# First stage rebuilt: six loads on ScalarE's queue, a tied filter chain, and all four quarters of v ahead of the gate products

## The chip, the cores and the metric

The kernel runs on one core of one Trainium2 chip. The metric is the device time of one execution in microseconds (us), the median of several runs. The engines are named as in the profile: PE (TensorE), DVE (VectorE), ACT (ScalarE), POOL (GpSimd) and SP (SyncE, which here only issues DMAs). A DMA is issued by an engine's queue; its data moves on the core's 16 DMA engines.

## The reference, cut to what matters

One layer works on 640 tokens (128 of context, 512 of a latent grid) of width 1024. What the first stage of the kernel computes is this:

```python
mod = (silu(cond) @ ada_w + ada_b)              # shift1, scale1, gate1, shift2, scale2, gate2
h = x * (1.0 + scale1) + shift1
proj = h @ w_in                                  # q, f_fwd, f_bwd, i_raw, g_raw, hy, mg
q, f_fwd, f_bwd, i_raw, g_raw, hy, mg = split(proj)
o_a = hgrn2_mixer(q, f_fwd, f_bwd, i_raw, ...)   # v = heads(i_raw)
o_b = hyena_mixer(hy, p, row_len)                # long convolution by FFT filters
# hyena_filters: h = sin(freq * (h @ w + b)) three times, then h @ w4, times a window
gate_a, gate_b = split(sigmoid(mg))
mix = (gate_a * (o_a @ proj_a) + gate_b * (o_b @ proj_b)) @ w_out
x = layer_norm(ALPHA * x + gate1 * mix)          # then a SwiGLU with shift2, scale2, gate2
```

## The kernel before, in words

All matrix products of fp32 data are made of two parts: a value is split into a high part (a cast) and a low part (the rest), and a product takes three passes of PE (high by high, low by high, high by low). Names that end in h and l are such pairs: hTh and hTl of the modulated input h, wh and wl of a tile of weights, abh and abl, kth and ktl. The weights come in a stream: `issue` loads a raw tile of 512 KB on SP's queue, casts the high part (by the engine that the string HIE names) and subtracts for the low part (by the one that WSUB names in the first stage), three tiles in flight; LOOK says how far ahead of a unit of work its weights are prepared.

The function `start` writes the first stage in the order of the tokens of PLAN; a scheduler then places each instruction on its engine, in order there. The tokens: x0 to x4 load the five blocks of 128 tokens (tile xs) and T0 to T4 transpose them on PE. `mlp` is the filter network, three layers of a small matmul (f1, f2, f3, lines L495, L500, L506) with a sine behind each (a chain of DVE steps on tiles sa and sk, then the sine on ACT, L170). k0 to k2 load a table kt and split it into kth and ktl. L0 to L3 load the weights (w4) and the window (win) of one quarter of the filters; A is `kern_a`: ks matmuls (L543), products with the window on DVE (af), and the split into abh (ACT) and abl (POOL or DVE). B is `kern_b`: matmuls kp and k (L572, L585) against kth and ktl, whose results go to tiles ko by DVE and ACT and are stored by W. D0 to D3 load the modulation's weights, each as two tiles of 1 MB (araw, three buffers), and M0 to M3 multiply and finish them (ada, adaT, modT). h0 to h7 make hTh and hTl. V0 and V1 are `v_unit`: one quarter of v is 120 matmuls of 256 columns (L708). e0 and e2 are `m1_operands`: sums and differences of the h tiles on DVE (mb) and their low parts (m4l to m7l), for products in the Winograd manner. `g0` and the tokens behind it make these gate products (ma, mb, mc, L668), whose weights (rm) are added and split on DVE and ACT as well (wmg0h, wmg0l, wma0l, wmu0l and so on).

Before, two quarters of v are made in the first stage and two (v2 v3 in HGSEQ) in the stage of the HGRN mixer. All loads of the first stage are issued by SP, small parameters by POOL, and the rows of c and c_ctx come with the parameters in one tile prow2. `ada_mods` is placed at high priority. A DMA's completion is counted in one of eight slots, DMAHW0 to DMAHW7, which are given round robin to the DMAs of SP's and ACT's queues; a DMA whose slot is still held waits at its issue until the earlier DMA has landed.

## Time and profile before

| | us |
|---|---|
| median of 3 runs | 1432.4 (1431.38 to 1432.75) |
| the profiled execution | 1434.48 |
| its span in the profile | 1431.4, at a granted PE clock of 0.993 |
| PE busy, DVE busy, ACT busy, POOL busy | 1379.5, 992.7, 620.5, 63.5 |

The profiled execution is 2.1 us above the median, and its span is 3.1 us below its own time. PE is busy for 96% of the span, so that 52 us are left in which it waits; a stage costs what its PE work takes and what PE waits there. Busy times of matmuls overlap, and the time that one really adds is the distance between two starts.

### The profile page before, as it was taken

The numbers are of one execution on the slowest core, as the hardware profiler recorded it, in microseconds if no ns is written. First come the engines' busy times: TensorE is split into PE (matmuls) and PEld (weight loads), VectorE is DVE, ScalarE is ACT, GpSimd is POOL, SyncE is SP. The second block draws the span as 40 slices with busy tenths as digits, with TensorE's granted clock in tenths as the row PEclk, the third lists the DMA queues.
The fourth block names the chain that finished last, engine by engine and source line by source line (L and its number), as shares of the span: only waits on it lengthen the run. The fifth ranks groups of instructions, "written<-read, shape, count | busy, mean of one in ns | idle before, by whom it ended". The sixth has DMA issues, their size and how long they took to land. (4 is left out here: it accounts for less than half of the span.)

```text
span 1431.4 us, 23426 instructions
## 1 busy us (share of the span) xinstructions
PE 1379.5 (96%) x9513; PEld 1294.7 (90%) x9513; DVE 992.7 (69%) x1751; ACT 620.5 (43%) x1011; POOL 63.5 (4%) x56
## 2 busy tenths in 40 slices
...
GB/s 239 334 140 141 207 212 183 199 247 162 93 97 102 113 230 142 144 84 81 76 95 62 68 68 139 221 115 78 88 132 116 78 116 108 83 189 281 74 60 74
DMA packets 198855, 195.63 MB, mean 137 GB/s; under 512 B 7581, under 2 KB 155773, under 8 KB 197980
## 3 DMA queue, kind: packets, MB, share of 16 engines
...
## 5 line engine op out<-in xcount | busy, mean ns | idle before, releaser
L181 DVE TENSOR_TENSOR wl<-raw,wh 128x1024 fp32r<-128x1024 f32 x96 | 117.2, 1223 | 132.9 <-ACT wh L357 132.0
L357 ACT CAST wh<-raw 128x1024 fp32r<-128x1024 f32 x90 | 94.2, 1049 | 221.2 <-PE pb L611 40.9
L1424 PE MATMUL fo<-wh,act 128*128 128x512 f32 (+1 forms) x440 | 130.6, 380 | 0.0
L1424 PEld LDWEIGHTS fo<-wh,act 128*128 128x128 f32 x440 | 81.2, 188 | 15.9
L1424 PE MATMUL fo<-wl,act 128*128 128x512 f32 (+1 forms) x220 | 83.4, 379 | 0.0
L611 PE MATMUL hy<-hTh,wh 128*128 128x320 f32 x256 | 79.6, 311 | 0.0
L611 PE MATMUL hy<-hTh,wl 128*128 128x320 f32 x256 | 79.1, 309 | 0.0
L611 PE MATMUL hy<-hTl,wh 128*128 128x320 f32 x256 | 79.1, 309 | 0.0
L611 PE MATMUL f<-hTh,wh 128*128 128x320 f32 x224 | 70.7, 316 | 0.0
L611 PE MATMUL f<-hTl,wh 128*128 128x320 f32 x224 | 69.7, 311 | 0.0
L611 PE MATMUL f<-hTh,wl 128*128 128x320 f32 x224 | 69.2, 309 | 0.0
L181 POOL TENSOR_TENSOR y<-y,gb 128x512 f32<-128x512 f32 x8 | 11.6, 1452 | 907.4 <-ACT y L170 907.1
L1424 PEld LDWEIGHTS fo<-wl,act 128*128 128x128 f32 x220 | 41.3, 188 | 7.9
L611 PEld LDWEIGHTS hy<-hTh,wh 128*128 128x128 f32 x256 | 48.1, 188 | 0.0
L611 PEld LDWEIGHTS hy<-hTl,wh 128*128 128x128 f32 x256 | 48.1, 188 | 0.0
L611 PEld LDWEIGHTS hy<-hTh,wl 128*128 128x128 f32 x256 | 48.1, 188 | 0.0
L170 ACT ACT_TABLE_LOAD x36 | 46.2, 1283 | 1.4 <-PEq L1770 0.7
L708 PE MATMUL v<-wl,hTh 128*128 128x256 f32 x160 | 45.2, 286 | 1.6 <-DVE wl L181 1.6
L708 PE MATMUL v<-wh,hTl 128*128 128x256 f32 x160 | 45.3, 285 | 0.1
L708 PE MATMUL v<-wh,hTh 128*128 128x256 f32 x160 | 45.1, 286 | 0.0
L611 PEld LDWEIGHTS f<-hTl,wh 128*128 128x128 f32 x224 | 42.2, 188 | 0.0
L611 PEld LDWEIGHTS f<-hTh,wh 128*128 128x128 f32 x224 | 42.2, 188 | 0.0
...
## 6 DMA issues: line engine op xcount, KB each, us to landing
...
```

Source lines behind the costliest of these rows:

```text
L170: r = S.activation(out, in_, func, bias=bias, scale=scale)
L181: return (eng or V).tensor_tensor(out=out, in0=a, in1=b, op=op)
L357: (V.tensor_copy if HIE[i] == "V" else S.copy)(hi, raw)
L611: r = PE.matmul(ps[:, 0:HT], w[a][:, k, :], x[b][:, k, c0:c0 + HT], start=k == 0 and i == 0, stop=k == kt - 1 and i == 2)
L708: PE.matmul(ps[:, (t - t0) * 256:(t - t0) * 256 + 256], hT[b][:, k, t * P:t * P + P], w[a][:, k % 4, :], start=k == 0 and i == 0, stop=k = ...
L1424: PE.matmul(ps, x(t, b, k0 + kk), w[a][:, kk, :], start=first and kk == 0 and i == 0, stop=last and kk == nk - 1 and i == 2)
```

## The change

In the first stage, blocks 0, 4 and 3 of x and three of the eight modulation tiles (a0, a1 and a4; a token a now loads one tile of 1 MB) are issued by ScalarE's queue, and so are the rows of c and c_ctx, in a tile crow that is transposed on its own (`cond_T`). Three instructions are tied in order to a place in the filter network's chain, without a wait: the first modulation matmul behind f3, the first of the two operations on w4 behind the clamp of the second layer, and the casts of kth behind the last sine. All casts of kth and of the first stage's weights are ACT's, all low parts of these weights DVE's. The modulation's multiplications (M) and its finish (Y) are tokens of their own, at no special priority. All four quarters of v stand in the first stage, among the quarters of the filters, and none in the HGRN stage. The tiles ko lie in the buffers of araw and xs, and no longer in those of the weights.

```diff
-PLAN = """x0 k0 L0 k1 x4 k2 p mlp t L1 T0 x3 T4 A0 x2 D0 T2 A1 x1 L2 B0 M0 T1 D2 A2 M2 T3 h0 L3 B1 D1 A3 h1 B2 M1 D3 h2 h3 M3 h4 W2 W0 h5 h6 h7 W1 q V0 e0 B3 g0 W3 V1 m w0 e2 ..."""
-HMOD = "SVSSVSSS"
+PLAN = """x0 a0 x4 a1 x3 a4 c mlp L0 k0 k1 p t T0 T4 T3 x1 x2 k2 a5 M0 M1 Y0 A0 L1 a2 M4 M5 Y2 T1 T2 a3 a6 B0 M2 M3 Y1 a7 h0 h1 h2 h3 A1 M6 M7 Y3 h4 h5 h6 h7 V0 W0 L2 B1 A2 V1 W1 L3 B2 V2 A3 W2 q B3 e0 g0 W3 V3 m w0 e2 ..."""
+HMOD = "SSSSSSSS"
-WSUB = "VGGVVGGG"
+WSUB = "VVVVVVVVVVVV"
...
-HIE = """SSSSVVSVSVSSSSSSSVVVSVVSVSSVSSSS..."""
-LOOK = """2222201220210220112012211122222..."""
+HIE = """SSSSSSSSVVSVSVSSSSSSSVVVSVVSVSSV..."""
+LOOK = """2222222220122021022011201221112..."""
-HGSEQ = """a0 b0 q0 g0 e0 v2 v3 a1 b1 q1 g1 s0 e1 ..."""
+HGSEQ = """a0 b0 q0 g0 e0 a1 b1 q1 g1 s0 e1 ..."""
...
-COPIES = {..., 'k': 'VSS', ...}
+COPIES = {..., 'k': 'SSS', ...}
...
     def tt(out, a, b, op, eng=None):
         return (eng or V).tensor_tensor(out=out, in0=a, in1=b, op=op)
+
+    def order_after(ins, prev):
+        if prev is not None:
+            tc.add_manual_dep(
+                ins.ins, prev.ins.name,
+                mybir.DependencyInfo(mybir.DependencyClass.NoSync, mybir.DependencyReason.DATA),
+                reason="issue order")
     def cpy(which, i, out, in_):
...
     prow1 = sp.tile([P, P], F32, name="prow1")
-    prow2 = sp.tile([65, P], F32, name="prow2")
+    prow2 = sp.tile([49, P], F32, name="prow2")
+    crow = sp.tile([16, P], F32, name="crow")
+    S.dma_start(crow[0:8], I["c_ctx"].rearrange("(k p) -> k p", p=P))
+    S.dma_start(crow[8:16], I["c"].rearrange("o (k p) -> (o k) p", p=P))
     skp_all = sp.tile([1, D], F32, name="skp_all")
     def params_load():
-        G.dma_start(prow2[49:57], I["c_ctx"].rearrange("(k p) -> k p", p=P))
-        G.dma_start(prow2[57:65], I["c"].rearrange("o (k p) -> (o k) p", p=P))
         G.dma_start(skp_all, I["hy_skip"])
...
         G.dma_start(msk, I["msk"])
-    def params_T():
-        ps = tr_bank("pr3_ps")
-        PE.transpose(ps[:, 0:65], prow2, ident[0:65, 0:65])
-        V.tensor_copy(cT.rearrange("p a k -> p (a k)"), ps[:, 49:65])
+    def cond_T():
+        ps = tr_bank("pr2_ps")
+        PE.transpose(ps[:, 0:16], crow, ident[0:16, 0:16])
+        V.tensor_copy(cT.rearrange("p a k -> p (a k)"), ps[:, 0:16])
         act(csig, cT, AF.Sigmoid)
...
             tt(scT[:, :, a:a + 1].rearrange("p k a -> p a k"), cT[:, a:a + 1, :], csig[:, a:a + 1, :], ALU.mult)
+
+    def params_T():
+        ps = tr_bank("pr3_ps")
+        PE.transpose(ps[:, 0:49], prow2, ident[0:49, 0:49])
         V.tensor_copy(prT2, ps[:, 0:49])
...
     modT = cp.tile([P, 4, KT, 2], F32, name="modT")
     ada = dict(raw={}, ps={})
+    net = {}
     def ada_load(nb, i, q, tag, bufs, eng=SY):
...
         for g in range(4):
-            PE.matmul(ps[32 * g:32 * g + 32, :], scT[:, 4 * i + g, :], raw[:, g, :], start=i == 0, stop=i == 1)
-
-    def ada_mods(nb, q):
-        with tc.high_priority():
-            for i in range(2):
-                ada_quad(nb, i)
-            ada_vec(nb, q)
+            r = PE.matmul(ps[32 * g:32 * g + 32, :], scT[:, 4 * i + g, :], raw[:, g, :], start=i == 0, stop=i == 1)
+            if (nb, i, g) == (0, 0, 0):
+                order_after(r, net["f3"])
     def ada_vec(nb, q):
...
     def x_load(t):
         xs = se.tile([P, D], F32, tag="xs", bufs=3, name=f"xs{t}")
-        SY.dma_start(xs, x_tok[t])
+        (SY if t in (1, 2) else S).dma_start(xs, x_tok[t])
         return xs
     def x_transpose(t, xs):
...
         V.scalar_tensor_tensor(a, k, MAGIC, a, ALU.subtract, ALU.subtract)
-        V.tensor_scalar(a, a, HALF, -HALF, ALU.min, ALU.max)
-        act(a, a, AF.Sin, scale=-TWO_PI)
+        net["clamp", nm] = V.tensor_scalar(a, a, HALF, -HALF, ALU.min, ALU.max)
+        net["sin", nm] = act(a, a, AF.Sin, scale=-TWO_PI)
         return a
     hf_hi = sp.tile([P, T], F32R, name="hf_hi")
...
             rs = slice(hf * ORD, hf * ORD + ORD)
-            PE.matmul(ps[:, 0:HT], w3[rs].rearrange("p a n -> p (a n)"), h2[rs], start=True, stop=True)
+            net["f3"] = PE.matmul(ps[:, 0:HT], w3[rs].rearrange("p a n -> p (a n)"), h2[rs], start=True, stop=True)
             h3 = sin_layer(ps[:, 0:HT], 2, f"3{hf}")
...
         SY.dma_start(raw, I["kt"][:, cs])
-        cpy("k", i, kth[:, cs], raw)
+        order_after(S.copy(kth[:, cs], raw), net["sin", "31"])
         tt(ktl[:, cs], raw, f32(kth[:, cs]), ALU.subtract, G if KSUB[i] == "G" else V)
     def kern_load(cc):
...
         wsd = se.tile([P, 2, 256], F32, tag="wsd", name=f"wsd{cc}")
-        tt(wsd[:, 0], w4[:, 0], w4[:, 1], ALU.add)
+        first = tt(wsd[:, 0], w4[:, 0], w4[:, 1], ALU.add)
+        if cc == 0:
+            order_after(first, net["clamp", "2"])
         tt(wsd[:, 1], w4[:, 0], w4[:, 1], ALU.subtract)
...
         kth_ = (kth, ktl)
-        def kout(n, nm):
-            if cc < 2:
-                t = wp.tile([P, n, 2, 256], F32, tag=("wh", "wl")[cc], bufs=HL_BUFS, name=f"ko{cc}_{nm}")
-            else:
-                t = sp.tile([P, n, 2, 256], F32, tag="ko", bufs=1, name=f"ko{cc}_{nm}")
-            return t
+        ko = se.tile([P, 2, 2, 2, 256], F32, tag="araw", bufs=3, name=f"ko{cc}")
         pk = o_bank(f"kp{cc}")
...
                           start=i == 0, stop=i == 2)
-        t = kout(1, "p")
+        t = se.tile([P, 1, 2, 256], F32, tag="xs", bufs=3, name=f"kop{cc}")
         cpy("o", 3 * cc, t[:, 0], pk.rearrange("p (x n) -> p x n", x=2))
...
             od = pk[1].rearrange("p (x n) -> p x n", x=2)
-            t = kout(2, kt)
+            t = ko[:, kt]
             tt(t[:, 0], od, ev, ALU.add)
...
             KQ.dma_start(kd[cc, :, f:f + n], t)
-
-    def order_after(ins, prev):
-        if prev is not None:
-            tc.add_manual_dep(
-                ins.ins, prev.ins.name,
-                mybir.DependencyInfo(mybir.DependencyClass.NoSync, mybir.DependencyReason.DATA),
-                reason="issue order")
     def dense_fm(w, x, half, ps, kt=KT, after=None):
...
     def v_unit(p):
         def fn(wa, wb):
-            v = (vp if p < 2 else hg["p"]).tile([P, NB, 256], F32, tag="v", bufs=1 + p // 2, name=f"v{p}")
+            v = vp.tile([P, NB, 256], F32, tag="v", bufs=1, name=f"v{p}")
             for t0 in range(0, NB, 2):
...
         U(v_unit(p), w_tm(w_in, 0, 4, COL_I + p * 256, 256), w_tm(w_in, 4, 4, COL_I + p * 256, 256))
-    v_add(0)
-    v_add(1)
+    for p in range(4):
+        v_add(p)
     vu = units[:]
     del units[:]
     def start():
-        stream["stop"] = 4
+        stream["stop"] = 8
         xs, ld, ab = {}, {}, {}
         def step(op, i):
...
                 ktab(i)
-            elif op == "D":
-                for n in range(2):
-                    ada_load(i, n, se, "araw", 3)
+            elif op == "a":
+                ada_load(*divmod(i, 2), se, "araw", 3, S if i in (0, 1, 4) else SY)
             elif op == "Q":
...
             elif op == "M":
-                ada_mods(i, se)
+                ada_quad(*divmod(i, 2))
+            elif op == "Y":
+                ada_vec(i, se)
             elif op == "h":
...
             else:
-                dict(p=params_load, t=params_T, q=params)[op]()
+                dict(p=params_load, c=cond_T, t=params_T, q=params)[op]()
         for tok in PLAN.split():
```

On ACT, the first instructions of the program were these before (sa are the filter network's tiles, wsd the sums of w4, kt the table):

```order
L170 ACT_TABLE_LOAD
L170 ACTIVATE sa1_175<-sa1_175 128x320 [waits DVE_49]
L184 CAST whi0_262<-wsd0_259 128x512 [waits DVE_49]
L184 CAST kth_135<-kt1_150 128x768 [waits DMAHW5_49]
L170 ACTIVATE sa2_185<-sa2_185 128x320 [waits DVE_49]
L184 CAST kth_135<-kt2_156 128x768 [waits DMAHW7_49]
L184 COPY xT0_129<-xT0_0_229 128x2x128 [waits PE_49]
```

After the change, ACT's first instructions are these (csig is the sigmoid of the conditioning; the names of tiles end in the program's own numbers):

```order
L297 DMA crow_118<-in_c_ctx 8x128
L298 DMA crow_118<-in_c 8x128
L459 DMA xs0_142<-in_x_prompt 128x1024
L410 DMA araw0_0_144<-in_ada_w 128x4x512 [waits DMAHW0_49]
L459 DMA xs4_146<-in_x_sample 128x1024 [waits DMAHW6_49]
L410 DMA araw0_1_148<-in_ada_w 128x4x512 [waits DMAHW0_49]
L459 DMA xs3_150<-in_x_sample 128x1024 [waits DMAHW4_49]
L410 DMA araw2_0_152<-in_ada_w 128x4x512 [waits DMAHW6_49]
L170 ACT_TABLE_LOAD
L170 ACTIVATE csig_105<-cT_104 128x16 [waits DVE_49]
L170 ACT_TABLE_LOAD
L170 ACTIVATE sa1_163<-sa1_163 128x320 [waits DVE_49]
```

Eight DMA issues stand ahead of the first sine (sa1), five of them with a wait for one of the eight slots, and a second table load; before, none stood there.

On DVE, around the last quarter of the filters (ko3) and the operands of the gate products, before:

```order
L181 TENSOR_TENSOR mb3_0_1078<-mb3_0_1078,mb0_0_1075 128x640
L181 TENSOR_TENSOR m5l_1068<-mb0_0_1075,m5h_1067 128x640
L181 TENSOR_TENSOR m7l_1072<-mb1_0_1076,m7h_1071 128x640
L181 TENSOR_TENSOR m6l_1070<-mb3_0_1078,m6h_1069 128x640
L181 TENSOR_TENSOR mb2_0_1077<-mb2_0_1077,mb3_0_1078 128x640
L181 TENSOR_TENSOR mb0_2_1341<-hTh1_842,hTl1_843 128x640
L181 TENSOR_TENSOR wmg0l_1169<-rm0_0_1166,wmg0h_1168 128x1024
L181 TENSOR_TENSOR wl3_1178<-raw3_1175,wh3_1177 128x1024
L181 TENSOR_TENSOR m4l_1074<-mb2_0_1077,m4h_1073 128x640
L181 TENSOR_TENSOR mb1_2_1342<-hTh1_842,hTl1_843 128x640
L181 TENSOR_TENSOR ko3_0_1132<-k3_0_1_1105,ev3_0_1130 128x512
L181 TENSOR_TENSOR ko3_0_1132<-ev3_0_1130,k3_0_1_1105 128x512
```

And after:

```order
L181 TENSOR_TENSOR ko3_1343<-k3_0_1_1354,ev3_0_1379 128x512
L181 TENSOR_TENSOR ko3_1343<-ev3_0_1379,k3_0_1_1354 128x512
L181 TENSOR_TENSOR ko3_1343<-k3_1_1_1384,ev3_1_1409 128x512
L181 TENSOR_TENSOR ko3_1343<-ev3_1_1409,k3_1_1_1384 128x512
L181 TENSOR_TENSOR wma0l_1601<-rm1_0_1598,wma0h_1600 128x512
L181 TENSOR_TENSOR mb0_0_1425<-hTh0_511,hTl0_512 128x640
L181 TENSOR_TENSOR mb1_0_1426<-hTh0_511,hTl0_512 128x640
L181 TENSOR_TENSOR mb2_0_1427<-hTh2_608,hTl2_609 128x640
L181 TENSOR_TENSOR mb3_0_1428<-hTh2_608,hTl2_609 128x640
L181 TENSOR_TENSOR mb0_0_1425<-mb1_0_1426,mb0_0_1425 128x640
L181 TENSOR_TENSOR rm1_0_1598<-rm1_0_1598 128x512
L181 TENSOR_TENSOR mb1_0_1426<-mb3_0_1428,mb1_0_1426 128x640
```

The operands mb and m4l to m7l stood ahead of the last ko3 and between them, and stand behind all four of them and behind wma0l now. The low part wmg1l stands 33 rows behind the last ko3.

On PE, in the HGRN stage, around the first transposes kT0_0 of the keys (t6), ahead of which the gate g1 of the second group of columns stood before:

```order
L611 MATMUL g1_1_6615<-hTh3_888,wh37_6464 128x320
L611 MATMUL g1_1_6615<-hTl3_889,wh37_6464 128x320
L611 MATMUL g1_1_6615<-hTh3_888,wl37_6465 128x320
L1233 MATMUL kT0_0_6646<-cst_84,t6_0_6150 128x128 x4
L1233 MATMUL kT0_1_6653<-cst_84,t6_0_6150 128x128 x4
L1242 MATMUL scp0_6660<-t4_0_6148,t5_0_6149 128x128
```

And after:

```order
L610 MATMUL f1_1_1_6552<-hTl3_619,wh36_6366 128x320
L610 MATMUL f1_1_1_6552<-hTh3_618,wl36_6367 128x320
L1233 MATMUL kT0_0_6645<-cst_84,t6_0_6429 128x128 x3
L610 MATMUL g1_0_6587<-hTh0_511,wh37_6463 128x320
L610 MATMUL g1_0_6587<-hTl0_512,wh37_6463 128x320
L610 MATMUL g1_0_6587<-hTh0_511,wl37_6464 128x320
L610 MATMUL g1_0_6587<-hTh0_511,wh37_6463 128x320
```

Three of these transposes stand ahead of the matmuls of g1_0 now, directly behind f1_1.

More of the change, by code (lines that the diff above doesn't have):

```diff
@@ L116, in _constants @@
     return {k: np.ascontiguousarray(v) for k, v in c.items()}
-PLAN = """x0 k0 L0 k1 x4 k2 p mlp t L1 T0 x3 T4 A0 x2 D0 T2 A1 x1 L2 B0 M0 T1 D2 A2 M2 T3 h0 L3 B1 D1 A3 h1 B2 M1 D3 h2 h3 M3 h4 W2 W0 h5 h6 h7 W1 q V0 e0 B3 g0 W3 V1 m w0 e2 10 20 g1 50 11 60 g2 70 21 30 40 w1 w2 61 51 52 12 71 Q8 62 22 g3 w3 13 41 g4 53 72 Q9 42 31 63 w4 g5 23 14 w5 73 Z4 Q10 43 32 g6 w6 64 24 15 54 74 Q11 33 65 25 44 16 26 55 75 Q12 Z5 g7 34 w7 66 45 56 17 76 Q13 35 67 46 g8 27 57 w8 18 77 Z6 Q14 g9 g10 36 w9 28 19 68 37 29 58 78 Q15 69 47 59 w10 79 Q16 38 110 210 Z7 g11 610 49 111 510 39 48 w11 211 g12 611 112 w12 212 710 Q17 g13 511 711 Q18 410 113 w13 311 612 Z8 310 411 512 712 Q19 513 213 613 412 713 312 413 313 Z9"""
-HMOD = "SVSSVSSS"
+PLAN = """x0 a0 x4 a1 x3 a4 c mlp L0 k0 k1 p t T0 T4 T3 x1 x2 k2 a5 M0 M1 Y0 A0 L1 a2 M4 M5 Y2 T1 T2 a3 a6 B0 M2 M3 Y1 a7 h0 h1 h2 h3 A1 M6 M7 Y3 h4 h5 h6 h7 V0 W0 L2 B1 A2 V1 W1 L3 B2 V2 A3 W2 q B3 e0 g0 W3 V3 m w0 e2 10 20 g1 50 11 60 g2 70 21 30 40 w1 w2 61 51 52 12 71 Q8 62 22 g3 w3 13 41 g4 53 72 Q9 42 31 63 w4 g5 23 14 w5 73 Z4 Q10 43 32 g6 w6 64 24 15 54 74 Q11 33 65 25 44 16 26 55 75 Q12 Z5 g7 34 w7 66 45 56 17 76 Q13 35 67 46 g8 27 57 w8 18 77 Z6 Q14 g9 g10 36 w9 28 19 68 37 29 58 78 Q15 69 47 59 w10 79 Q16 38 110 210 Z7 g11 610 49 111 510 39 48 w11 211 g12 611 112 w12 212 710 Q17 g13 511 711 Q18 410 113 w13 311 612 Z8 310 411 512 712 Q19 513 213 613 412 713 312 413 313 Z9"""
+HMOD = "SSSSSSSS"
 HSUB = "GVVVVGVG"
-WSUB = "VGGVVGGG"
+WSUB = "VVVVVVVVVVVV"
 TAILPOS = 1
```

8 lines of the change are left out of this document (4 added, 4 removed).

## The prediction

> **What bounds the kernel now.** I read the page's busy times first, then PE's waits by releaser in the first 180 us, then the windows of 20 us, then single rows.
>
> ```profile
> span 1431.4 us, 23426 instructions
> PE 1379.5 (96%) x9513; PEld 1294.7 (90%) x9513; DVE 992.7 (69%) x1751; ACT 620.5 (43%) x1011; POOL 63.5 (4%) x56
> ```
> ```profile
> PE k L585 <- DVE af L181: 2.0, 1, 2.0
> PE mc L668 <- ACT wmu1h L619: 0.8, 1, 0.8
> PE mc L668 <- DVE wmu0l L181: 0.3, 1, 0.3
> ```
> ```profile
> 0.00:20.00 20.00, 5.76 (x21) 2.83 (x22) 9.55 (x24) 4.80 (x8) 12.77 (x22) 1.00 0.76 223
> 20.00:40.00 20.00, 15.63 (x72) 10.20 (x71) 17.12 (x40) 10.99 (x26) 3.61 (x3) 0.91 0.80 278
> 40.00:60.00 20.00, 18.48 (x132) 13.54 (x132) 18.54 (x37) 11.18 (x25) 7.91 (x5) 1.00 0.86 305
> 60.00:80.00 20.00, 16.89 (x124) 12.84 (x122) 14.09 (x28) 13.04 (x21) 9.20 (x5) 1.00 0.86 294
> 100.00:120.00 20.00, 20.00 (x165) 20.00 (x164) 18.61 (x26) 9.46 (x15) 0.00 (x0) 1.00 0.34 126
> ```
>
> A window's row is its length, the busy time of PE, its weight loads, DVE, ACT and POOL, PE's granted clock, DMA share and GB/s. PE idles 52 us in all (1431.4 less 1379.5), and 23.2 us of it in the first 80 us (80 less 5.76, 15.63, 18.48 and 16.89), while DMA is at 0.76 to 0.86. From 100 us on PE is full, and gate products begin with only 1.1 us of waits (the mc rows). So moving v's matmuls is worth nothing in itself: the change wins what it fills of PE's holes in the start, and loses what its order opens elsewhere. I add up three places: the HGRN stage, the start up to the first gate product, and the first gate products.
>
> ```profile
> L708 PE MATMUL v<-wh,hTh x80: 280/283/415, 71.6 to 116.4; 128*128 128x256 f32 x80
> L668 PE MATMUL ma<-hTh,wmg0h x4: 309/309/312, 116.7 to 118.1; 128*128 128x320 f32 x4
> 73.69 0.28 PE L708 MATMUL v<-wh,hTh 128*128 128x256 f32 x1
> 73.81 0.28 PE L708 MATMUL v<-wh,hTl 128*128 128x256 f32 x1
> L708 PEld LDWEIGHTS v<-wh,hTh x80: 188/192/192, 568.0 to 597.4; 128*128 128x128 f32 x80
> 597.89 0.31 PE L611 MATMUL f<-hTh,wh 128*128 128x320 f32 x1
> 598.04 0.31 PE L611 MATMUL f<-hTl,wh 128*128 128x320 f32 x1
> ```
>
> The third numbers of the rows with x80 and x4 are first and last start. By the distances of starts a matmul of 256 columns adds 0.12 us, one of 320 columns 0.15; I take 0.235 for 512 columns, about twice the first. The first v starts at 71.6, the first gate product at 116.7; v2 and v3 run from 568.1 to the next f at 597.9.
>
> **Term 1, the HGRN stage.** 240 matmuls leave it, with a short wait inside: 29.8 us. They were also cover: DVE and ACT worked on the first gates' chain meanwhile.
>
> ```profile
> 583.40 0.48 DVE L181 TENSOR_TENSOR t<-t,xx 128x320 f32<-128x320 f32 x1
> 619.02 0.38 PE L1233 MATMUL kT<-cst,t 128*128 128x128 f32 x2
> ```
> ```profile
> 80.25 0.39 PE L585 MATMUL k<-abh,kth 128*128 128x256 f32 x1 [2.04 <-DVE af L181]
> 81.06 0.41 PE L585 MATMUL k<-abh,ktl 128*128 128x256 f32 x1
> 81.27 0.41 PE L585 MATMUL k<-abh,kth 128*128 128x256 f32 x1
> 84.24 0.28 PE L708 MATMUL v<-wh,hTl 128*128 128x256 f32 x1
> ```
>
> The keys' transposes kT ran at 619.0, long after their t was done near 583.9. They stand directly behind f1_1 now, 96 matmuls of 320 columns (14.1 us) behind the old start of v2: PE is there at about 582.3. The DVE chain that makes t is the same, with another tile's low part now ahead of the step: I put t at 584.4, a wait of 2.1 us. A wait has a tail, which the second fence shows: after 2.04 us idle, the matmuls of 256 columns start 0.21 apart until about 84.2, so some 17 to 19 of them lose 0.09 each, 1.7 us. Term 1 is −29.8 + 2.1 + 1.7 = −26.0, with bounds −29.8 (t is in time) and −22 (one more stall of that size).
>
> **Term 2, the first v.** 106 rows stand ahead of it on PE now (196 before): one filter quarter and the ks of two more; the last of these rows are the eighth modulation tile's matmuls and transposes. So its landing sets the start.
>
> ```profile
> DMA  0231699999999999999980029999998029999999
> GB/s 0 62 60 41 164 382 283 248 350 394 401 238 236 376 257 376 403 400 390 408 198 1 0 55 341 354 397 321 389 333 337 19 74 348 257 255 380 410 408 403
> DMA packets 9962, 16.12 MB, mean 269 GB/s; under 512 B 1340, under 2 KB 5148, under 8 KB 9959
> 58.49 0.37 SPq L397 DMA_DIRECT2D araw<-in_ada_w  x1
> DMA to landing us min/median/max: 8.1/8.2/8.3
> 67.95 1.06 PE L406 MATMUL ada<-araw,scT 128*32 128x512 f32 x8
> 71.62 0.28 PE L708 MATMUL v<-wh,hTh 128*128 128x256 f32 x1
> ```
>
> The first three rows are the DMA in 40 slices of the first 60 us: full from about 6 us, with two holes, near 30 to 35 and 46 to 48 us. The last modulation tile was issued at 58.5, landed at 66.7 (8.2 later), and the first v started 4.9 us behind that, since h had still to be made. The 16.1 MB of those 60 us are also about what must have come by the same landing after the change (five blocks of x, eight modulation tiles, the table, two windows, the first filter weights and three tiles for v). Without a hole, at 370 GB/s (an estimate from the full slices, 236 to 410), they take 43.5 us from about 5 us: landed at 48.5. Behind it come the last matmuls, a copy and a transpose, 2.5 us, since the h that v0 needs first is ready earlier: T = 51. Bounds: 44 (all at 410 GB/s and an order by which the last tile isn't last), and 58, if the loads' hand-over of buffers opens a hole of 4 us as before and the rest is slow.
>
> That the holes don't come back isn't certain, because ScalarE's queue is blocked now.
>
> ```profile
> 8.12 0.47 ACT L170 ACTIVATE sa<-sa 128x320 f32<-128x320 f32 x1 [6.10 <-DVE sa L483]
> 10.76 0.56 DVE L184 CAST kth<-kt 128x768 fp32r<-128x768 f32 x1 [2.67 <-DMA kt<-in_kt]
> 12.10 1.73 DVE L181 TENSOR_TENSOR wsd<-w 128x256 f32<-128x256 f32 x2 [0.78 <-DMA w<-in_filt_w]
> 17.07 1.44 PE L506 MATMUL f<-sa,w 64*128 64x320 f32 x4 [7.10 <-ACT sa L170]
> 20.93 0.98 SPq L397 DMA_DIRECT2D araw<-in_ada_w  x2
> ```
>
> Of ACT's first eight instructions five wait for an earlier landing, and its sines stand behind them. x4 is issued once c is there, near 4 us, a4 once x4 is there, some 8 us later; so the first sine, at 8.1 before, starts near 13. But the second layer was held up before too: DVE stood 2.7 us for kt and 0.8 for w4 ahead of it (rows at 10.76 and 12.10), and f3 ran at 17.1. One of the two operations on w4 is still ahead, untied; the kth cast isn't. I put f3 at 17.4 to 18.8, so the blocked queue costs 0 to 2 us at the chain's end. The casts of kth behind the last sine put POOL's three ktl ahead of its first abl, and the first filter quarter some 5 us later than it could be; PE's second modulation tile, whose buffer the eighth one takes, stands behind that quarter. This is why I take 370 GB/s and not 410.
>
> From the first v to the first gate product stand 642 matmuls of 256 columns (480 of v, 162 of kp and k) and 20 ks: 642 × 0.121 + 20 × 0.235 = 82.4 us, all of them, since none has another place. I add 4 us for holes, two of the size of the one at 80.25 with its tail halved (h and the third modulation part are made in that stretch). The first gate product then starts at 51 + 82.4 + 4 = 137.4, against 116.7: +20.7, with bounds +14 and +28.
>
> **Term 3, the first gate products.** The low parts and the operands (mb, m4l to m7l) of e0 and e2 stand behind ko3 on DVE now, in order, and ko3 waits for PE's k matmuls, 82 matmuls ahead of the first gate product, 9.7 us.
>
> ```profile
> L181 DVE TENSOR_TENSOR mb<-mb,mb 128x640 f32<-128x640 f32 x8 | 6.5, 811 | 0.0
> L181 DVE TENSOR_TENSOR m4l<-mb,m4h 128x640 fp32r<-128x640 f32 x2 | 1.6, 821 | 0.8 <-ACT m4h L619 0.8
> L181 DVE TENSOR_TENSOR wmg1l<-rm,wmg1h 128x1024 fp32r<-128x1024 f32 x1 | 1.2, 1219 | 0.0
> L181 DVE TENSOR_TENSOR ko<-k,ev 128x512 f32<-128x512 f32 x3 | 2.0, 681 | 0.0
> ```
>
> Four ko at 0.6, six of 512 columns behind them, 23 of 640 at 0.74 (0.81 busy, of which the next one overlaps some 0.07, as the row at 583.40 overlaps its next), two of 1024 at 1.14 and one small one: 26 us, and some 1.5 us of waits for ACT's high parts. The last, wmg1l, is done at 137.4 − 9.7 + 27.7, 18 us behind the first gate product; PE wants it 8.5 us behind it, and loses 9.6 us where it lost 1.1 before; with a tail of 1 us +9.5. Bounds: +1 (DVE is ahead after all), +11 (the store of v, which now has one buffer, and the modulation tile behind it in that buffer wait as well).
>
> The rest costs nothing: the low parts of eight weight tiles are 1.2 us each on DVE, in windows that leave it 1.5 to 5.9 us in 20; a POOL that does none was hidden; the separate transpose of crow is one matmul in PE's empty first 20 us; the later stages have the same order.
>
> **The sum.** −26.0 + 20.7 + 9.5 = +4.2 us. The profiled execution at 1434.48 becomes 1438.7; the median lies 2.1 below it, so 1432.4 becomes 1436.6.
>
> **The rivals.** *The DVE backlog is hidden (faster).* Term 3 is +1 and the sum −4.3: 1428.1. For it: even with both operands and these weights in it, the window of 100 to 120 us left DVE 1.4 us free, and the operands need only h. Against: DVE runs in order, and four ko that wait for PE stand ahead. It decides where term 3 falls below 5.3 us, that is where wmg1l is done before 14 us behind the first gate product. Faster by 0.2% needs term 3 under 2.4, or the first v at 44. *The loads stay the bound (slower).* Two queues don't make the transfers faster; if the holes return with the buffers and ScalarE's blocked sines delay the filters, T = 57 and the sum is +10: 1442.6. For it: the full slices before, and the five slot waits. Against: the modulation tiles start at 6 to 8 us and not at 20.9. [...] *It doesn't do what it says (no better than a plain move).* If the first v isn't reached earlier than PE's rows require, v's 59.4 us are only moved: start and HGRN cancel up to 3.8, and term 3 comes on top, +13: 1445.7. Against: PE has 52 us of holes, and 90 rows fewer stand ahead of v.
>
> **How the numbers follow.** 0.2%, 2.9 us, is about what a measurement of this kernel can tell from no change. Chances: my forecast 0.42 (own range 1430 to 1441), the hidden backlog 0.32, the loads 0.16, the plain move 0.10. Faster: 0.9 of the hidden backlog and a tenth of the forecast, 0.34. Within 0.2%: a third of the forecast, and what is left of the rival, 0.18. Slower: the rest, 0.48. The range of 8 in 10 goes from 1424 (hidden backlog with T at 47) to 1446.
>
> **What would show it.** In the profile after: the first v between 48 and 54; the first gate product near 137; DVE's ko3 directly ahead of mb, and PE's mc waiting for DVE's m and wm tiles for some 9 us behind it; a wait of kT on DVE's t of 2 us, and no v in HGRN; no DMA slice under 5 tenths before 45 us. I am wrong if PE runs through the gate products without those waits, or if the first v comes at 44 or 58.

## The result and the profile after

The changed kernel takes 1446.1 us (median of 4 runs, 1445.05 to 1447.03), the kernel before 1431.9 beside it: ratio 1.0104, 95% interval 1.0092 to 1.0116. The profiled execution took 1447.0 us; its span is 13.7 us longer than before's. The page of the changed kernel, its busy times:

```profile
span 1445.1 us, 23441 instructions
PE 1380.5 (96%) x9514; PEld 1294.9 (90%) x9514; DVE 995.2 (69%) x1751; ACT 623.1 (43%) x1016; POOL 49.3 (3%) x49
```

PE has the same work; what grew is its idle time, 51.9 to 64.6 us. PE's waits in the first 200 us, by releaser (total, times, longest):

```profile
PE pr_ps L283 <- DMA frow<-in_filt_b: 8.5, 1, 8.5
PE f L509 <- ACT sa L170: 8.3, 1, 8.3
PE ma L667 <- ACT wmg2h L618: 3.5, 1, 3.5
PE k L591 <- POOL abl L181: 3.2, 4, 1.5
PE ada L419 <- DMA araw<-in_ada_w: 2.5, 2, 1.5
PE f L515 <- ACT sa L170: 2.5, 1, 2.5
PE xT L466 <- DMA xs<-in_x_sample: 1.6, 1, 1.6
PE mc L667 <- ACT wmu0h L618: 1.6, 1, 1.6
```

The 7.1 us ahead of f3 are gone (2.5 now), but the first matmul of all waits 8.5 for frow, the filter network's frequencies and biases (4.7 before), and f2 waits 8.3 for the first sine (2.5 before). Behind them new waits stand at the gate products (ma, mc). Where v and these products start, and kT's wait in HGRN:

```profile
L707 PE MATMUL v<-wh,hTh x160: 274/283/365, 59.3 to 146.6; 128*128 128x256 f32 x160
L667 PE MATMUL ma<-hTh,wmg0h x4: 309/309/312, 146.9 to 148.2; 128*128 128x320 f32 x4
623.51 0.87 PE L1233 MATMUL kT<-cst,t 128*128 128x128 f32 x3 [2.26 <-DVE t L181]
```

Three anchors split the difference. They are first starts on PE in the two profiled executions: the first gate product (ma), the first hy matmul of the next stage, the first fo matmul near the end.

| stretch | before | after | moved by |
|---|---|---|---|
| start to first ma | 116.7 | 146.9 | +30.2 |
| first ma to first hy | 194.4 | 203.1 | +8.7 |
| first hy to first fo | 959.8 | 934.7 | −25.1 |

The two quarters of v were 29.8 us in HGRN. The start grew by as much. So the rebuilt first stage hides nothing of them: PE is busy there for 25.5 us more, and its idle time grew too, by this row of each kernel (length, then PE's busy time, and PE's clock ahead of the DMA share). Before:

```profile
0.00:116.70 116.70, 93.06 (x631) 75.52 (x632) 94.24 (x182) 60.09 (x108) 39.17 (x37) 0.97 0.66 223
```

After:

```profile
0.00:146.90 146.90, 118.52 (x872) 102.09 (x873) 85.15 (x164) 64.96 (x116) 32.46 (x33) 0.99 0.61 201
146.90:166.00 19.10, 12.41 (x66) 8.93 (x64) 18.73 (x26) 11.83 (x18) 0.00 (x0) 0.91 0.60 198
```

Idle ahead of ma: 23.6 us before, 28.4 after. In the 19 us behind it PE idles 6.7 us while DVE is full: the debt of the operands' work.

### The profile page after: what moved, and what is told of

Same layout as the page of the kernel before. It is cut to its first block, busy times and chain, and to the rows that moved or that the text cites. A ratio compares the mean times of both kernels' runs of the same rounds, so it can differ in the third digit from the quotient of the medians.

```text
span 1445.1 us, 23441 instructions
## 1 busy us (share of the span) xinstructions
PE 1380.5 (96%) x9514; PEld 1294.9 (90%) x9514; DVE 995.2 (69%) x1751; ACT 623.1 (43%) x1016; POOL 49.3 (3%) x49
## 5 line engine op out<-in xcount | busy, mean ns | idle before, releaser
L181 DVE TENSOR_TENSOR wl<-raw,wh 128x1024 fp32r<-128x1024 f32 x101 | 123.3, 1223 | 127.0 <-ACT wh L369 123.4
L369 ACT CAST wh<-raw 128x1024 fp32r<-128x1024 f32 x90 | 94.2, 1048 | 215.1 <-PE pb L610 41.0
L170 ACT ACT_TABLE_LOAD x36 | 46.2, 1283 | 15.8 <-DMA xs<-in_x_sample 15.1
L1424 PEld LDWEIGHTS fo<-wl,act 128*128 128x128 f32 x220 | 41.3, 188 | 7.9
L610 PEld LDWEIGHTS f<-hTh,wl 128*128 128x128 f32 x224 | 42.1, 188 | 0.0
```

The lines of the kernel that those rows point to most:

```text
L170: r = S.activation(out, in_, func, bias=bias, scale=scale)
L181: return (eng or V).tensor_tensor(out=out, in0=a, in1=b, op=op)
L369: (V.tensor_copy if HIE[i] == "V" else S.copy)(hi, raw)
L610: r = PE.matmul(ps[:, 0:HT], w[a][:, k, :], x[b][:, k, c0:c0 + HT], start=k == 0 and i == 0, stop=k == kt - 1 and i == 2)
L1424: PE.matmul(ps, x(t, b, k0 + kk), w[a][:, kk, :], start=first and kk == 0 and i == 0, stop=last and kk == nk - 1 and i == 2)
```

## The experiments

Times are medians; the kernel before stood at 1431.3 to 1431.9 beside them. The first ma of kernels with the same start differs by up to 2.6 us between profiled executions, so smaller shifts are not read. In the tables below, "ma" is its start, "gate" the stretch from ma to hy less before's 194.4, "rest" that from hy to fo less before's 959.8. These stretches come from one profiled execution each, the times from all executions; where the two disagree, the text says so. The granted clock in a window is the mean of the clock's records, which begin at 16 to 35 us; a window ahead of the first record shows 1.00.

### Who holds up the start: e1, e2, e3

```diff
 e1: (SY if t in (1, 2) else S).dma_start(xs, x_tok[t])   ->  SY.dma_start(xs, x_tok[t])
     ada_load(..., S if i in (0, 1, 4) else SY)            ->  ada_load(...)
 e2: G.dma_start(frow...)                                  ->  S.dma_start(frow...)   # three loads, ahead of crow and x0
 e3: KSUB = "GGG"                                          ->  KSUB = "VVV"
```

> All of the change, but x0, x4, x3 and a0, a1, a4 are issued by SP again, in the same order; only the rows of c stay with ScalarE. Theory 'blocked queue' (ScalarE's sines wait behind its own DMA issues until 15.1 us): the first sine goes from 17.95 us to 9 to 13, f3 from 22.3 to 15 to 18, the first ks from 29.6 to 25, the first v from 59.3 to about 54, the time from 1446.1 to about 1441. Rival 'transfers' (the loads themselves are the bound, whoever issues them): the first v within 1.5 us of 59.3, the time 1445 to 1447.

> All of the change, but the three small loads of frow (the filter network's frequencies and biases) that POOL issued are issued by ScalarE ahead of x0 and a0. Theory 'blocked queue': frow lands some 4 us earlier and f1 runs near 5 us instead of 8.9, but the first sine stays where ScalarE comes free, 16 to 18 us, and the time stays within 1.5 us of 1446.1. Rival 'late small rows' (the large loads push frow back, and the network's whole chain with it): the first sine 4 us earlier, first v 55, time about 1442.

> All of the change, but the three ktl subtractions are DVE's and not POOL's. Theory 'POOL holds up DVE' (three DVE steps with two SBUF operands took 1.4 to 2.1 us instead of 0.4 to 0.5 while POOL ran ktl): these three steps fall back to 0.4 to 0.5, DVE gains 4.1 and pays 3 times 0.9, the first v comes 1 to 4 us earlier, 1442 to 1445. Rival 'DVE has room there': the three ktl are only added, 2.7 us, first v later by 0 to 3, 1446 to 1449.

| | time | ratio, interval | first sine | f3 | ks | first v | ma |
|---|---|---|---|---|---|---|---|
| before | 1431.9 | | 8.1 | 17.1 | 23.7 | 71.6 | 116.7 |
| the change | 1446.1 | 1.0104 (1.0092 to 1.0116) | 18.0 | 22.3 | 29.6 | 59.3 | 146.9 |
| e1 | 1445.2 | 1.0091 (1.0074 to 1.0108) | 8.5 | 12.8 | 26.5 | 60.4 | 146.3 |
| e2 | 1454.7 | 1.0165 (1.0147 to 1.0182) | 25.2 | 29.5 | 37.6 | 66.9 | 153.6 |
| e3 | 1447.6 | 1.0110 (1.0095 to 1.0125) | 17.6 | 21.9 | 29.4 | 59.4 | 147.5 |

That ScalarE's issues block its sines is plain in the changed kernel's rows of ACT (start, duration, the last one's wait in brackets):

```profile
14.72 0.39 ACTq L410 DMA_DIRECT2D araw<-in_ada_w  x1
15.13 1.28 ACT L170 ACT_TABLE_LOAD   x1 [15.13 <-DMA xs<-in_x_sample]
17.95 0.47 ACT L170 ACTIVATE sa<-sa 128x320 f32<-128x320 f32 x1
```

The last issue leaves at 14.7 us, two table loads follow, and the sine is 9.8 us later than before. In e2 three more DMAs shift the slots, and the last issue waits till 21.9:

```profile
21.91 0.39 ACTq L410 DMA_DIRECT2D araw<-in_ada_w  x1
25.15 0.47 ACT L170 ACTIVATE sa<-sa 128x320 f32<-128x320 f32 x1
```

There f3, first v and ma are all later by 6.7 to 7.6 us, and the time by 8.6. I had expected the block to stay where it was; it grew instead, and showed that a delay of the sines goes through to the end nearly one for one. But the way back isn't open: in e1 the sines run at 8.5 and f3 9.5 us earlier, and ma comes 0.6 us earlier. The blocked queue is real, and taking it away wins nothing by itself. The first v stayed, as the rival had it, and loads have a part in that. PE waits for v's weights there, and their cast for their landing:

```profile
60.35 0.39 PE L707 MATMUL v<-wh,hTh 128*128 128x256 f32 x1 [2.02 <-ACT wh L369]
59.26 1.05 ACT L369 CAST wh<-raw 128x1024 fp32r<-128x1024 f32 x1 [2.26 <-DMA raw<-in_w_in]
```

SP issues these weights at 49.4 us, behind the eighth modulation tile (48.9), which waits for its buffer; in the changed kernel they were issued at 41.4, ahead of it. And as in e8 below, PE's idle time ahead of ma falls (28.4 to 21.5 us) while the same work is busy for longer (118.5 to 124.8).

In e3 the three stretched DVE steps do shrink. The changed kernel's DVE, while POOL runs ktl from 31.4 to 37.3:

```profile
31.65 1.95 DVE L181 TENSOR_TENSOR hf_lo<-sa,hf_hi 64x320 fp32r<-64x320 f32 x1
35.51 0.67 DVE L181 TENSOR_TENSOR af<-ks,win 128x512 f32<-128x512 f32 x1
36.12 1.43 DVE L561 SCALAR_TENSOR_TENSOR af<-af,skp_all 1x256 f32<-1x256 f32 x1
```

And e3's:

```profile
30.79 0.47 DVE L181 TENSOR_TENSOR hf_lo<-sa,hf_hi 64x320 fp32r<-64x320 f32 x1
31.19 2.68 DVE L181 TENSOR_TENSOR ktl<-kt,kth 128x768 fp32r<-128x768 f32 x3
35.95 0.41 DVE L561 SCALAR_TENSOR_TENSOR af<-af,skp_all 1x256 f32<-1x256 f32 x1
```

1.95 becomes 0.47 and 1.43 becomes 0.41, but the three ktl cost DVE 2.7 us, the first v stays at 59.4, and the time doesn't fall, as the rival had it. The stretching is shown, its price on the path is none that can be measured.

### Small loads first: e8, and all together: e10

```diff
 e8 = e1, and
-PLAN = """x0 a0 x4 a1 x3 a4 c mlp L0 k0 ...
+PLAN = """L0 x0 a0 x4 a1 x3 a4 c mlp k0 ...
 e10 = e8 and e9 (below)
```

> As e1 (the six loads on SP's queue), and w4 and the window of the first filter quarter are issued ahead of them, not behind. Theory 'small loads behind large ones' (the start's chain waits for frow and w4, which share the DMA engines with x and the modulation tiles that are issued before them): ks at 18 to 21 us instead of 26.5 and 29.6, first v at 50 to 54, time 1437 to 1441. Rival 'PE and the transfers set the first v' (PE has 34 us of work ahead of it, and the eighth modulation tile must land): ks 18 to 21, but the first v at 57 to 60, time 1443 to 1446.

> e8 and e9 together. If the start's chain sets the first v, 1429 to 1434, no slower than the kernel before; if PE's work and the transfers do, 1436 to 1440.

e8: 1446.5 us, ratio 1.0103 (1.0083 to 1.0122); f3 at 12.6, ks at 23.3 (so the 18 to 21 expected weren't reached), first v at 63.1 (later than either theory had it), ma at 145.7. e10: 1441.0, ratio 1.0071 (1.0055 to 1.0088), 1 us above its second case; ma at 145.5. The start's chain is 6 to 10 us earlier in e8 and ma 1.2. Its windows tell where that went (the first row is the changed kernel's, the others are e8's):

```profile
30.00:60.00 30.00, 24.47 (x160) 15.26 (x160) 25.21 (x46) 21.23 (x38) 10.53 (x6) 0.94 0.91 307
30.00:60.00 30.00, 23.31 (x117) 15.22 (x117) 21.66 (x37) 16.35 (x32) 8.45 (x6) 0.72 0.77 246
32.90:43.10 10.20, 8.33 (x36) 5.86 (x36) 4.77 (x6) 3.30 (x8) 3.28 (x2) 0.50 0.88 293
53.40:60.20 6.80, 6.06 (x27) 3.21 (x28) 6.50 (x13) 4.12 (x8) 1.56 (x2) 0.50 1.00 347
0.00:145.70 145.70, 123.87 (x872) 104.91 (x873) 88.56 (x164) 65.65 (x116) 31.82 (x33) 0.94 0.61 202
```

PE's idle time ahead of ma falls from 28.4 to 21.8 us, as wanted. But the same 872 matmuls are busy for 123.9 us instead of 118.5, at a granted clock of 0.72 in 30 to 60 us (0.94 in the changed kernel): the clock stood at 0.50 for 17 us of e8's way to ma, and for 3.4 us of the changed kernel's. At half the clock the 13.6 us between them cost at most half, 6.8 us (an estimate from these rows). The work came earlier, in pieces with waits between, and ran slower: 6.6 us won, 5.4 given back.

What lowers the clock isn't shown. The longest wait of PE between 20 and 60 us of e8 is 2.03 us, and in 40 to 60 us PE idles 3.8 us of e3 at a granted clock of 1.00 and 3.1 us of e8 at 0.76 (e3's row, then e8's):

```profile
40.00:60.00 20.00, 16.22 (x118) 11.23 (x117) 17.39 (x32) 16.48 (x30) 2.87 (x2) 1.00 0.83 280
40.00:60.00 20.00, 16.91 (x90) 9.63 (x88) 14.09 (x28) 11.67 (x21) 3.14 (x3) 0.76 0.62 201
```

### Is PE full ahead of v: e13, e17

```diff
 e17 = e9, and
-... a3 a6 B0 M2 M3 Y1 a7 h0 ...
+... a3 a6 M2 M3 Y1 a7 B0 h0 ...
 e13 = e9, and with tc.high_priority() around ada_quad (M) and ada_vec (Y) of the first stage
```

> e9 (ko3 apart, kT tied), and the modulation's second part (M2, M3) is written ahead of the first filter quarter's products, so that PE runs ada1 amid them and not behind them. Theory 'buffer hand-over': the eighth modulation tile is issued at 42 to 45 us instead of 48.4, the first v at 51 to 54 instead of 56.7, the first gate product 3 to 5 us earlier than e9's 144.3, the time 1436 to 1438. Rival 'PE is full there': the issue is earlier but the first v stays within 1.5 us of 56.7 and the time within 1.5 of 1440.6.

> e9 (ko3 apart, kT tied), and the modulation's matmuls and finish in the first stage are placed at high priority again, as before the change; ada1 then stands ahead of most of the first filter quarter's k matmuls. Theory 'buffer hand-over' (the eighth modulation tile is issued only when ada1 has run behind those k matmuls, at 48.4 to 51.7 us): it is issued at 40 to 45, the first v comes at 50 to 54 instead of 56.7, the time falls by 3 to 6 from 1440.6. Rival 'PE's work sets the first v': the issue is earlier, the first v stays at 55 to 58, 1439 to 1442.

e17: 1440.9 us, ratio 1.0065 (1.0053 to 1.0078), against e9's 1440.6. The rival wins. The eighth modulation tile is issued at 41.3 us instead of 48.4 (51.7 in the changed kernel), and the first v comes at 56.2 against 56.7. Rows of e17, SP's issue, then PE's first v, then two windows:

```profile
41.27 0.37 SPq L410 DMA_DIRECT2D araw<-in_ada_w  x1
56.16 0.36 PE L707 MATMUL v<-wh,hTh 128*128 128x256 f32 x1
0.00:34.00 34.00, 14.90 (x74) 9.54 (x75) 17.12 (x45) 12.19 (x26) 12.45 (x20) 1.00 0.97 311
34.00:144.60 110.60, 104.51 (x801) 94.50 (x799) 72.59 (x125) 54.37 (x92) 20.03 (x14) 0.98 0.50 166
```

From 34 us to ma PE is busy for 104.5 of 110.6 us. The landing of the eighth tile, on which my start time rested, is not what the first v waits for; 19 of the 25 us of idle time lie ahead of 34 us. In the changed kernel PE does wait for that landing, but for 1.04 us only. Its rows, with the windows up to f3, from f3 to the first v, and of the loads' first 54.4 us:

```profile
57.13 1.07 PE L419 MATMUL ada<-araw,scT 128*32 128x512 f32 x8 [1.04 <-DMA araw<-in_ada_w]
0.00:22.30 22.30, 2.98 (x10) 0.89 (x10) 6.07 (x22) 3.77 (x6) 7.12 (x17) 1.00 0.86 286
22.30:59.30 37.00, 31.47 (x199) 19.85 (x200) 29.57 (x60) 25.98 (x53) 10.53 (x6) 0.95 0.95 302
0.00:54.40 54.40, 31.34 (x185) 19.62 (x185) 30.74 (x72) 26.17 (x54) 17.65 (x23) 0.97 0.91 294
```

PE is idle for 19.3 us up to f3, and from f3 to v stand 31.5 us of its work with 5.5 us of waits, 37.0 in all. In the other kernels that keep these loads on ScalarE (e2, e3, e4, e5, e9, e17, f2) this distance is 36.0 to 37.5 us, whenever f3 comes, from 19.6 to 29.5 us. So there the sines set f3, and f3 sets v. With the loads on SP it doesn't hold (47.6 us in e1, 50.5 in e8), and whether e17's order would have helped those two wasn't tried out. e13 (1443.8, 1.0062 to 1.0091) issued that tile at 48.9 and had ks at 37.1, since the modulation's matmuls and transposes, now first on PE, ran ahead of it and waited 1.8 us for their tiles; first v at 62.7, ma at 152.9. Both theories of e13 missed.

### v alone, and the rest without it: f1, e4, f2

```diff
 (each with the strings of the weight stream and the buffers of v that go with it)
 f1: the kernel before, and
-... h7 W1 q V0 e0 B3 g0 W3 V1 m ...      HGSEQ ... e0 v2 v3 a1 ...
+... h7 W1 q V0 V1 e0 B3 V2 g0 W3 V3 m ...   HGSEQ ... e0 a1 ...
 e4: the change, and V2 and V3 out of PLAN, v2 v3 back in HGSEQ
 f2: e4 and e5 (below)
```

> The kernel before, and of the change only that all four quarters of v stand in the first stage (V1 and V2 around the last filter quarter, V3 ahead of the gate products), with the weight stream's strings that go with it. Theory 'plain move': first v at 71 to 73, first gate product at 145 to 147, kT's wait in HGRN 2 to 4 us, the time 1434 to 1437. Rival 'v as cover' (in the changed kernel taking the two quarters back cost 10 us, so bringing them must win): 1424 to 1430.

> All of the change, but the third and fourth quarter of v are back in the HGRN stage (with the strings of the weight stream that go with it). Theory 'plain move' (the first stage's holes are as large as before, so 29.1 us of PE's work are only moved; the price is kT's wait in HGRN, 2.3 us with its tail 4, and the order at the gate products): the first v stays at 59 to 60, the first gate product comes at 117 to 119, kT waits for nothing, the time is about 1442 (1440.5 to 1443.5). Rival 'v fills holes' (the two quarters hide 5 us or more of the start's waits): first gate product at 122 or later, 1446 to 1450.

> e4 (v2 and v3 back in the HGRN stage) with ko3 in its own buffer and e0 ahead of the last filter quarter. Theory 'cover' (e4 was 10 us slower than the changed kernel because the two quarters of v cover the operands' DVE work that stands behind ko3): with the operands ahead, that price falls by 8 to 14 us, the time to 1442 to 1449. Rival 'the start itself is worse' (the rebuilt start costs that much whatever DVE's order): within 3 us of e4, 1453 to 1459.

| | time | ratio, interval | ma | gate | rest |
|---|---|---|---|---|---|
| the change | 1446.1 | 1.0104 (1.0092 to 1.0116) | +30.2 | +8.7 | −25.1 |
| f1, v alone | 1439.0 | 1.0045 (1.0029 to 1.0061) | +28.9 | +1.7 | −25.2 |
| e4, all but v | 1456.4 | 1.0172 (1.0151 to 1.0192) | +6.1 | +20.7 | +0.5 |
| f2, e4 with ko3 apart | 1455.4 | 1.0159 (1.0143 to 1.0175) | +9.1 | +10.1 | +0.7 |

f1 is the plain move: 28.9 us come to the start, 25.2 leave HGRN, 1.7 are lost at the gate products, +5.4 in its profile and +7.4 in the medians (above the 1434 to 1437 expected). Its kT waits 2.3 us, as in the changed kernel.

e4 missed both ways: I expected it 4 us faster than the change, or at most 4 slower, and it is 10 us slower. Without the two quarters the rebuilt stage loses 20.7 us at the gate products: 12.2 are idle time, and 8.5 the longer busy time of the same work at a lower clock (0.95 and not 1.00), by the rows from ma to hy of the kernel before and of e4:

```profile
116.70:311.10 194.40, 192.29 (x1294) 176.58 (x1294) 131.67 (x216) 99.04 (x171) 5.11 (x2) 1.00 0.63 196
122.80:337.90 215.10, 200.79 (x1293) 181.61 (x1293) 152.96 (x245) 103.90 (x179) 0.00 (x0) 0.95 0.56 174
```

e4's waits there:

```profile
PE ma L667 <- ACT wms0h L618: 3.8, 1, 3.8
PE ma L667 <- ACT wmg2h L618: 3.5, 1, 3.5
PE ada L419 <- DMA araw<-in_ada_w: 3.3, 1, 3.3
PE mc L667 <- ACT wmu0h L618: 1.9, 1, 1.9
```

f2 stayed within 3 us of e4 in the medians (1.0 us), as its rival had it. In the profiled executions its gate products lose 10.6 us less than e4's and ma comes 3.0 later; but these two lie 4.0 us above e4's median and 2.5 below f2's, so the shift can't be sized from them. f2's windows show a limit: DVE is full in 120 to 140 us (19.9 of 20), while it had 8 to 9 us free in 60 to 80 and in 80 to 100:

```profile
60.00:80.00 20.00, 19.23 (x154) 18.50 (x154) 11.18 (x16) 11.90 (x21) 7.91 (x5) 1.00 0.44 143
80.00:100.00 20.00, 20.00 (x160) 19.56 (x159) 12.01 (x18) 7.70 (x13) 5.29 (x3) 1.00 0.28 103
120.00:140.00 20.00, 10.88 (x55) 10.41 (x54) 19.86 (x30) 9.68 (x16) 0.00 (x0) 0.80 0.13 53
```

The rebuilt order puts DVE's work late: 85.2 us of it are done ahead of ma in the changed kernel, in 146.9 us, against 94.2 in 116.7 before. The change as a whole is better than its parts' sum (+24.5 and +7.4 against +14.2). That the two quarters of v cover a part of DVE's debt, and keep PE's work unbroken and its clock up (0.95 in e4's row), is how I read these rows; no run separates the two, and the theory of f2, that DVE's order at the operands is the price, missed.

### The price behind the start: e5, e9

```diff
 e5: -ko = se.tile([P, 2, 2, 2, 256], F32, tag="araw", bufs=3, ...)
     +the same for cc < 3; for cc == 3 two tiles sp.tile([P, 2, 2, 256], F32, tag="ko", bufs=1)
     -PLAN ... W2 q B3 e0 g0 ...
     +PLAN ... W2 q e0 B3 g0 ...
 e9: e5, and order_after(first kT transpose of head 0, last matmul of g1)
```

> All of the change, but the tiles ko3 lie in the small buffer that held them before, not in those of araw and xs, so that e0 can stand ahead of the last filter quarter (as in the kernel before). Theory 'order of DVE at the gate products' (ko3 ahead of e0 costs what PE waits behind the first gate product, 7.8 us with tails 8.7): these waits fall to 1 to 4 us and the time to 1439 to 1442. Rival 'the loads there are late' (rm and the modulation tile wait for v's store and its one buffer): PE's waits stay above 6 us, 1445 to 1447.

> All of the change, with ko3 in its own small buffer (as in e5) and the first transpose of kT tied behind g1's last matmul (as PE had them before). Both theories of the price behind the start (DVE's order at the gate products 3.5 us, kT's wait and tail 4 us) add up: 1438 to 1440. If kT's wait only moves to a later place (the next user of the same DVE chain), 1442 to 1444.

e5: 1443.6, ratio 1.0084 (1.0068 to 1.0100); gate +5.4 instead of +8.7. e9: 1440.6, ratio 1.0066 (1.0046 to 1.0085); gate +4.6, rest −28.5. e5's time lies between its two theories, e9's 0.6 us above its first. Of the gate products' waits in e9 these are left:

```profile
PE mc L667 <- ACT wmu0h L618: 2.3, 1, 2.3
PE ma L667 <- DVE wmg1l L181: 1.5, 1, 1.5
```

In the changed kernel these rows stood there, the largest wait of the gate products and what held its weights up:

```profile
157.98 1.04 ACT L618 CAST wmg2h<-rm 128x1024 fp32r<-128x1024 f32 x1 [2.02 <-DMA rm<-in_w_in]
159.08 0.42 PE L667 MATMUL ma<-hTh,wmg2h 128*128 128x320 f32 x1 [3.46 <-ACT wmg2h L618]
```

The place of the ko tiles is the cause of e0's place: with ko3 in the buffers of araw and xs, e0 can't stand ahead of it, since e0's tiles take the memory of those buffers. With ko3 out the gate products lose 3.3 to 4.1 us less in the profiles; the medians of e5 and the change lie 2.5 us apart, with intervals that overlap. With the tie kT's wait (2.3 us in e5) is gone, and g waits 1.3 us for ACT instead; the stretch behind hy is 3.4 us shorter than the change's and 1.0 shorter than e5's, and kernels without the tie differ there by as much (932.3 in e5, 935.6 in e8), so the tie alone isn't sized. Together, e9's two edits win 5.5 us of the medians. Where e9's last 8.8 us lie no trace shows: its profiled execution, 3.8 us below its median, is only 3.6 us longer in span than before's, with the start's +27.6 and the rest's −28.5 nearly cancelling and the gate's +4.6 left.

### The ties alone: g1, g2

```diff
 the kernel before, and
-cpy("k", i, kth[:, cs], raw)
+order_after(S.copy(kth[:, cs], raw), net["sin", "31"])      # g2: net["sin", "2"]
+order_after(first, net["clamp", "2"])                        # g2: both operations on w4
-PLAN = """x0 k0 L0 k1 x4 k2 p mlp t L1 ...
+PLAN = """x0 L0 x4 p mlp k0 k1 k2 t L1 ...
```

> The kernel before, and of the change only the ties: all kth casts are ScalarE's and tied behind the last sine, the first operation on w4 behind the second layer's clamp, and the table kt is loaded behind w4 and the window. Theory 'the tie is worth its wait' (DVE stood 3.5 us for kt and w4 ahead of the second layer's chain): f3 at 13 to 14.5 instead of 17.1, ks at 19 to 22 instead of 23.7, the first gate product 2 to 4 us earlier, 1427.5 to 1430. Rival 'the late table' (kth and POOL's ktl behind the last sine delay the first filter quarter, which is needed next): ks earlier, but the first gate product within 1.5 us of 116.7, 1430.5 to 1433.5.

> As g1, but the kth casts are tied behind the second layer's sine and not the last one, and both operations on w4 behind the second clamp. Theory 'the tie is worth its wait': f3 at 12.5 to 14, first gate product 3 to 5 us earlier than 116.7, 1426.5 to 1429.5. If the casts now hold up the last sines (ACT waits for kt's landing), f3 as in g1 but ks at 22 to 24 and the time 1430.5 to 1433.5.

g1: 1436.6, ratio 1.0034 (1.0022 to 1.0047). g2: 1435.2, ratio 1.0024 (1.0015 to 1.0034). The ties do what they say: f3 at 14.6 and 12.4 us instead of 17.1, ks at 20.6 and 20.7 instead of 23.7. Nothing of it arrives: ma at 117.5 and 116.2 against 116.7, and both kernels are slower than either theory of theirs had it. In g1 PE's idle time ahead of ma grew by 1.7 us. In g2 it fell by 1.8, but the work there was busy for 1.3 longer, at a lower granted clock in 20 to 40 us (0.74 and not 0.91); g2's window, which in the kernel before had 72 matmuls in 15.63 us of busy time:

```profile
20.00:40.00 20.00, 15.91 (x67) 9.60 (x68) 15.49 (x29) 10.55 (x24) 6.68 (x4) 0.74 0.87 307
```

Five matmuls fewer in slightly more busy time. What costs the last 3 us of g1 and g2 behind ma wasn't tried out.

## Why the prediction was wrong

It forecast slower by 4.2 us, 1436.6, in a range of 1424 to 1446; measured were +14.2 and 1446.1. The step that failed is term 2, the time of the first gate product: forecast +20.7, measured +30.2. The 9.5 us between them are nearly the whole difference. Within term 2 it is the start of the first v, T: forecast 51, set by the landing of the eighth modulation tile; measured 59.3, set by f3 and by PE's own work behind it.

- **Term 1 (HGRN).** −26.0 forecast, −25.1 measured in the changed kernel and −25.2 in f1. kT waits 2.26 us for t, as worked out (2.1).
- **Term 3 (gate products).** +9.5 forecast, +8.7 measured. DVE ran in order, the last ko3 at 138.65 and the first mb at 141.53, and its row of wmg1l stood at 164.36 to 165.57, 18.7 us behind ma (18 forecast). But PE takes wmg1l up only at 167.9 and doesn't wait for it; it waits 3.46 for ACT's wmg2h, which stood 2.02 for its weights' landing, 1.58 for wmu0h, 1.47 for a modulation tile, 0.80 for m6l and 0.36 for wms0h. Late loads were in the forecast for the upper bound only. So DVE's delay was right, the waits are others, and that the sum agrees is in part luck. The 3.3 to 4.1 us less of e5 and e9 would be a good third to a half of the term.
- **Term 2, its parts.** The first sine came at 18.0 and not near 13, f3 at 22.3 and not 17.4 to 18.8: frow landed 3.8 us later behind x0 and a0 (I had not costed that these large loads go ahead of a small one), and ScalarE was blocked to 15.1 and not to 12. ks followed 7.3 us behind f3 (6.6 before), with 24 transposes and 16 modulation matmuls between them on PE. The eighth tile was issued at 51.7, and PE took it up as it landed, at 57.1 and not at 48.5; v began at 59.3 and not 51. The last part held: from v to ma 87.6 us, forecast 86.4.
- **The error under these.** I took the landing of the eighth tile as the bound and never summed PE's own work ahead of v. The landing itself was mis-sized: at 370 GB/s the 16.1 MB were to have come by 48.5 us, and at the 294 GB/s of the first 54.4 us 16.0 MB had come by then. But the landing isn't the bound. With the tile issued 7.1 us earlier in e17 than in e9 PE waits for it no more (1.55 us in e9), and v moved 0.5; with f3 7.2 us later in e2, v moved 7.6. What holds is f3 plus 37 us: the blocked queue, priced at 0 to 2 us at the chain's end and in T only by the choice of 370 GB/s over 410, made f3 5.2 us later than before (22.3 against 17.1). To reach ma at 137.4 PE's idle time ahead of it, 23.6 us before, would have had to fall to 19 (137.4 less 118.5); no variant of the changed kernel came under 24.7 (e9) but those with the loads on SP (21.5 in e1, 21.8 in e8, 23.4 in e10), and these paid in busy time (124.8, 123.9 and 122.1 instead of 118.5).
- **The rivals.** The plain move, at 0.10 and 1445.7, comes nearest to what happened: start and HGRN cancel but for 5 us, and the gate products come on top. That its number fits is in part luck: the move alone costs 7.4 us in f1, and the rebuilt start without it 24.5 in e4. What spoke against it, "PE has 52 us of holes, and 90 rows fewer stand ahead of v", was no reason: fewer rows ahead of v don't shorten what must stand ahead of the gate products. The hidden backlog (0.32) did not occur. The loads as bound (0.16) came near in its number, T = 57, and the DMA engines were full (0.95 from f3 to v), and two queues moved no more than one (273 and 310 GB/s in the first two stretches of 20 us; 265 and 360 in e1, with these loads on SP), but e2 and e17 speak against its mechanism.

No kernel tried here beats the one before.
